# A routed transformer on one core: token tile 0 routed inside the query product, and repeated experts dropped instead of waited for

## The chip, the core and the metric

One core of one Trainium2 chip runs the whole program, in one launch. The metric is the device time of that launch in microseconds, as the median of several runs. The kernel before was run three times: 3288.59, 3291.32 and 3292.28 us, median 3291.32.

## The reference, cut to what matters

256 tokens of width 2048 go through a first block (two kinds of attention, then a routed feed-forward layer called PEER) and two further hybrid layers. All is float32. The change is in PEER alone:

```python
def peer_ffn(h, w_q, sub_keys, u, v):
    q = einsum('td,de->te', ht, w_q).reshape(T, 8, 2, 128)
    scores = einsum('thcd,hcnd->thcn', q, sub_keys)          # 8 heads, 2 halves, 128 keys
    s1, i1 = top_k(scores[:, :, 0], 16)
    s2, i2 = top_k(scores[:, :, 1], 16)
    cand_scores = (s1[..., :, None] + s2[..., None, :])       # 16 x 16 per head
    cand_idx = i1[..., :, None] * 128 + i2[..., None, :]
    top_scores, top_pos = top_k(cand_scores, 16)
    experts = take_along_axis(cand_idx, top_pos)              # 16 of 16384 per head
    gates = softmax(top_scores)
    ...
    a = einsum('td,thkd->thk', xb, u[eb])
    w = gb * gelu(a)
    return einsum('thk,thkd->td', w, v[eb])
```

Every token picks 8 x 16 = 128 experts out of 16384. Two heads of one token may pick the same expert; within one head the 16 are distinct.

## The kernel before, in words

**Weights and pieces.** The 256 tokens are two tiles of 128. All weights stream through in pieces of 1 MB (`raw`, three buffers). For each piece ScalarE (ACT) rounds it to `whi` (L155), VectorE (DVE) subtracts to get the remainder `wlo` (L156), and TensorE (PE) does three products (L180 to L182) for each of 4 row blocks and 2 token tiles, 24 matmuls in all. This L156 subtraction is called a split below, and splits are counted from the first one, which is split 0; split *n* is made two pieces ahead of its matmuls.

**What sets the order.** `chunk` runs a job of four pieces and calls `tick()` after each piece. A tick advances every running generator task by one step, in the order in which the tasks were spawned. Each engine works strictly in the program's order, so everything that a task issues between two `yield`s stands between two splits on DVE, and a row that waits holds up all rows behind it on its engine.

**The jobs around the change.** `peer_q(0..3)` (16 pieces) is the query product. After each of the four jobs, its task makes key scores for both tiles and then the top 16 of 128 for each score row (`top16`, L920 to L925; one such call is a *list*, and there are 4 lists for each job and tile). `route` is spawned after the last `peer_q`, and waits for all four. For each tile it goes through 8 heads: the 256 candidate sums (L939) and their top 16, then for each pair of heads a comparison on DVE (L955), a product on GpSimd (POOL, L959) and a reduction on DVE (L962), which give the expert's two halves. At the tile's end come the softmax, the expert numbers `ex` (L975) and the scatter addresses `au` (L977).

**The gate writes.** `scatter_gates(tt)` writes each token's gates to a dense table `gm[tt]` in DRAM: 128 indirect DMAs per tile, each issued by POOL, one column of 128 tokens per DMA (L991). Its value is the sum of the token's gates over all its copies of that expert, which DVE computes first (`same`, L1007). A tick issues four `same` and four scatters. A repeated expert is thus written more than once with the same value, at one address. Every sixteenth scatter therefore waits until the sixteen before it have landed:

```python
group.append(scatter("gates%d_%d" % (tt, k // 16), gm[tt], au[:, k:k + 1], total[:, k:k + 1],
                     group[k - 16:k] if k % 16 == 0 else ()))
```

Such a wait is called a drain below.

**Behind the gate writes.** `expert_u(0..31)` (128 pieces, splits 154 to 281) computes the activations of all experts and stores them (`wd`). `find_hits(tt)` reads `gm[tt]` back once all its 128 scatters have landed (SP issues the loads, L1026) and reduces them on DVE (L1030). After tile 1's, `list_experts` ranks the experts in use and scatters their numbers to a list `ls` in DRAM with 128 more indirect DMAs on POOL (L991 again), 4.5 per tick on average; experts not in use get an address beyond the bound (L1097, with `oob_is_err=False`, so that they are dropped). SP reads the list back (L1123) when all have landed, and DVE casts it (L1126 to L1128), before one certain split. `early_factors` multiplies gates into activations that were stored before the gates were known (L1055). Then follow `mem_kv` (8 pieces; its input tiles are rounded on ACT and subtracted on POOL, L1297, four times) and `expert_v`, whose rows POOL gathers by the list (L1185).

Of the kernel before, what the change touches and what calls it, by code (L numbers as in the profile page):

```python
# [14 lines left out]
OP = mybir.AluOpType  # L15
AX = mybir.AxisListType

P = 128
# [20 lines left out]
def tile_kernel(ctx, tc, a, o):  # L39
# [70 lines left out]
    jobs = []  # L110
# [100 lines left out]
    def pieces(ap, n=512):  # L211
        return [(ap[i], 4, n) for i in range(ap.shape[0])]
# [671 lines left out]
    def peer_q(c):  # L884


        def after(acc):
            tok = new([P, 2, 512])
            for tt in range(2):
                S.activation(tok[:, tt], acc[tt], AF.Copy, scale=st["rh"][:, tt:tt + 1])  # L890
            qT = new([P, 4, 256])

            def gen():
                yield
                transposes([[tok[:, tt, b * P:(b + 1) * P] for tt in range(2)] for b in range(4)],
                           lambda b0, nb, pt: S.copy(qT[:, b0:b0 + nb], pt))
                yield
                scs = []
                for tt in range(2):
                    p4 = psum("bs", (P, 4, P))  # L900
                    for b in range(4):
                        PE.matmul(p4[:, b], qT[:, b, tt * P:(tt + 1) * P], st["sk"][c // 2][:, 4 * (c % 2) + b],
                                  start=True, stop=True)
                    sc = new([P, 4, P])
                    S.copy(sc, p4)
                    scs.append(sc)
                yield
                for tt in range(2):
                    for b in range(4):
                        top16(slot["s"][:, tt, 4 * c + b], slot["i"][:, tt, 4 * c + b], scs[tt][:, b], P)  # L910
                        if b % 2:
                            yield
            st["pq", c] = spawn(gen())
        chunk(pieces(a["w_peer_q"][c]), lambda: st["h2"], after, before=peer_start if c == 0 else None)

    def top16(val, idx, src, n):

# [8 lines left out]

    def route():

        for c in range(4):
            while not st["pq", c].done:  # L930
                yield
        for tt in range(2):
            s, ix = slot["s"][:, tt], slot["i"][:, tt]
            ts, tp = new([P, 8, 16]), new([P, 8, 16])
            hi, lo = new([P, 8, 16]), new([P, 8, 16])
            i16 = st["iota"][:, :16]
            for h in range(8):
                cand = new([P, 16, 16])
                V.tensor_tensor(cand, s[:, 2 * h].unsqueeze(2).to_broadcast([P, 16, 16]),  # L939
                                s[:, 2 * h + 1].unsqueeze(1).to_broadcast([P, 16, 16]), op=OP.add)  # L940
# [17 lines left out]
                for which, eq in enumerate(eqs):  # L958
                    G.tensor_tensor(eq, eq, src[:, :, which].unsqueeze(2).to_broadcast([P, 2, 16, 16]), op=OP.mult)  # L959
                yield  # L960
                for eq, nm in zip(eqs, ("i1", "i2")):
                    V.tensor_reduce(slot[nm][:, tt, 16 * h0:16 * h0 + 32].rearrange("p (h k) -> p h k", h=2), eq,  # L962
                                    axis=AX.X, op=OP.add)
# [10 lines left out]
            ex, au, ad = slot["ex"][:, tt, 0], slot["au"][:, tt], new([P, P])  # L974
            V.scalar_tensor_tensor(ex, slot["i1"][:, tt], float(P), slot["i2"][:, tt], op0=OP.mult, op1=OP.add)  # L975
            V.tensor_scalar(ad, ex, float(P), st["token"], op0=OP.mult, op1=OP.add)
            V.tensor_copy(au, ad)  # L977
            st["scatter", tt] = spawn(scatter_gates(tt, ex, au, slot["ex"][:, tt, 1]))
            yield
# [17 lines left out]

    def scatter_gates(tt, ex, au, total):


        while tt and not st["scatter", 0].done:
            yield
        gt, group = slot["gt"][:, tt], []
        for k0 in range(0, P, 4):
            for k in range(k0, k0 + 4):
                same = new([P, P])
                V.scalar_tensor_tensor(same, ex, ex[:, k:k + 1], gt, op0=OP.is_equal, op1=OP.mult, accum_out=total[:, k:k + 1])  # L1007
            for k in range(k0, k0 + 4):
                group.append(scatter("gates%d_%d" % (tt, k // 16), gm[tt], au[:, k:k + 1], total[:, k:k + 1],
                                     group[k - 16:k] if k % 16 == 0 else ()))  # L1010
            yield
        yield
        st["group", tt] = group
        if tt == 0:
            st["hits"] = new([P, 2, P])
            spawn(find_hits(0, 1))

    def find_hits(tt, pace):

        yield  # L1020
        ready.append(tt)
        pend = []
        for d in range(16 + 2 * pace):
            if d < 16:
                gt = new([P, 8, P])
                after_all(nc.sync.dma_start(gt, gmp[tt][d]).ins, st["group", tt])  # L1026
                pend.append(gt)
            if d >= 2 * pace:
                e = d - 2 * pace
                V.tensor_reduce(st["hits"][:, tt, 8 * e:8 * e + 8], pend[e], axis=AX.X, op=OP.max)  # L1030
            if d % pace == pace - 1:
                yield
        st["factors", tt] = spawn(early_factors(tt))
# [586 lines left out]
    def layer(l):  # L1620
# [59 lines left out]
            chunk(pieces(w[8 + i]), xs2, z_gate(i), before=reload if i == 3 else None)  # L1680
        out2(l)

    for c in range(4):
        peer_q(c)
    jobs.append(lambda: st.__setitem__("route", spawn(route())))
    for c in range(32):
        expert_u(c)
    mem_kv(0)
# [102 lines left out]
```

## Time and profile before

| | value |
|---|---|
| median of three runs | 3291.32 us |
| the profiled execution | 3292.52 us |
| its span (first to last instruction) | 3290.7 us |
| PE busy / DVE / ACT / POOL | 95% / 59% / 45% / 34% |
| mean granted clock of PE | 0.98 |
| gate scatters on POOL | 256, mean 1312 ns |
| list scatters on POOL | 128, mean 1352 ns |

The profiled execution took 1.20 us more than the median of the runs. All times below are counted from the start of its span. A row's bracket gives the idle time of its engine just ahead of it, and what ended that; "idle before" in a grouped row is the sum of these. The work around the change lies between 860 us (query product) and 1960 us (first gathers).

### The profile page before, as it was taken

The numbers are of one execution on the slowest core, as the hardware profiler recorded it, in microseconds if no ns is written. First come the engines' busy times: TensorE is split into PE (matmuls) and PEld (weight loads), VectorE is DVE, ScalarE is ACT, GpSimd is POOL, SyncE is SP. The second block draws the span as 40 slices with busy tenths as digits, with TensorE's granted clock in tenths as the row PEclk, the third lists the DMA queues.
The fourth block names the chain that finished last, engine by engine and source line by source line (L and its number), as shares of the span: only waits on it lengthen the run. The fifth ranks groups of instructions, "written<-read, shape, count | busy, mean of one in ns | idle before, by whom it ended". The sixth has DMA issues, their size and how long they took to land. (4 is left out here: it accounts for less than half of the span.)

```text
span 3290.7 us, 38470 instructions
## 1 busy us (share of the span) xinstructions
PE 3139.9 (95%) x14755; PEld 2590.5 (79%) x14755; DVE 1935.2 (59%) x2441; ACT 1494.3 (45%) x1755; POOL 1128.1 (34%) x798
## 2 busy tenths in 40 slices
PE   8999999999999899994996899999999999999998
PEld 7888888888887778783785788887788888888886
DVE  5544455555589865861752466665675545665545
ACT  6566565443443344441442355555444443444542
POOL 1211121000002777676188688888200001000001
PEclk9999999999999999997998999999999999999999
DMA  7676455555644555993995587878644456644454
GB/s 258 203 256 223 156 183 191 204 205 204 221 167 167 175 193 171 338 321 93 371 371 208 186 293 288 287 279 302 240 177 150 164 196 239 216 157 161 153 204 154
DMA packets 172655, 717.56 MB, mean 218 GB/s; under 512 B 28865, under 2 KB 66178, under 8 KB 104114
## 3 DMA queue, kind: packets, MB, share of 16 engines
q1 hardware_dynamic: 138546, 583.57, 50.6%
q0 software_dynamic: 33920, 131.47, 11.4%
q8 instruction: 118, 1.93, 0.2%
q14 instruction: 71, 0.58, 0.0%
HBM read 659.38 MB, written 55.58 MB: 217 GB/s over the span
## 5 line engine op out<-in xcount | busy, mean ns | idle before, releaser
L156 DVE TENSOR_TENSOR wlo<-raw,whi 128x2048 fp32r<-128x2048 f32 (+3 forms) x521 | 1169.4, 2246 | 830.6 <-ACT whi L155 830.5
L181 PE MATMUL acc<-wlo,k 128*128 128x512 f32 (+3 forms) x3540 | 1372.0, 388 | 93.1 <-DVE wlo L156 93.1
L180 PE MATMUL acc<-whi,k 128*128 128x512 f32 (+3 forms) x3540 | 1398.5, 395 | 24.3 <-ACT whi L155 24.3
L182 PE MATMUL acc<-whi,k 128*128 128x512 f32 (+3 forms) x3540 | 1377.0, 389 | 0.0
L155 ACT CAST whi<-raw 128x2048 fp32r<-128x2048 f32 (+3 forms) x521 | 963.2, 1851 | 742.3 <-PE acc L182 440.4
L181 PEld LDWEIGHTS acc<-wlo,k 128*128 128x128 f32 x3540 | 671.0, 190 | 235.4 <-DVE wlo L156 100.0
L180 PEld LDWEIGHTS acc<-whi,k 128*128 128x128 f32 x3540 | 671.2, 190 | 153.6 <-ACT whi L155 24.7
L182 PEld LDWEIGHTS acc<-whi,k 128*128 128x128 f32 x3540 | 670.8, 189 | 144.6
L991 POOL DMA_INDIRECT gm<-k,k x256 | 335.8, 1312 | 138.5 <-issue 55.9
L991 POOL DMA_INDIRECT ls<-b,b x128 | 173.0, 1352 | 109.8 <-DVE b L1107 71.6
L1185 POOL DMA_INDIRECT k<-wd,b x111 | 195.1, 1757 | 37.9 <-issue 33.5
L223 POOL TENSOR_SCALAR b<-b 128x8 f32<-128x8 f32 (+1 forms) x22 | 6.9, 312 | 481.7 <-ACT b L257 241.5
L1519 POOL TENSOR_TENSOR k<-k,k 128x1024 f32<-128x1024 f32 x8 | 19.2, 2405 | 369.8 <-ACT k L1518 328.8
L1185 POOL DMA_INDIRECT raw<-peer_v_dram,b x73 | 119.4, 1636 | 46.9 <-issue 20.1
L1265 PE MATMUL acc<-whi,k 128*128 128x512 f32 x324 | 127.2, 393 | 4.7 <-DVEq L1220 3.0
L1266 PE MATMUL acc<-wlo,k 128*128 128x512 f32 x324 | 126.5, 391 | 0.0
L235 PE MATMUL bt<-ident,k 128*128 128x128 f32 x800 | 109.5, 276 | 5.5 <-DVE k L244 3.4
L156 DVE TENSOR_TENSOR wlo<-k,whi 128x2048 fp32r<-128x2048 f32 x38 | 87.1, 2292 | 41.9 <-ACT whi L155 41.8
L235 PEld LDWEIGHTS bt<-ident,k 128*128 128x128 f32 x800 | 93.9, 141 | 21.9 <-DVE k L244 4.9
L775 POOL TENSOR_TENSOR k<-k,k 128x1024 f32<-128x1024 f32 x8 | 19.3, 2415 | 262.5 <-ACT k L774 262.5
L1416 POOL COPY b<-k 128x128 f32<-128x128 f32 x4 | 8.9, 2222 | 276.5 <-DVE k L1414 276.5
L155 ACT CAST whi<-k 128x2048 fp32r<-128x2048 f32 x38 | 72.4, 1906 | 46.9 <-PE bs L1268 43.6
(363 smaller groups left out, 2803.2 us busy)
## 6 DMA issues: line engine op xcount, KB each, us to landing
raw<-w_dram SPq DMA_DIRECT2D x176, 1024.0 KB, 4.9
raw<-peer_u_dram SPq DMA_DIRECT2D x128, 1024.0 KB, 6.5
raw<-w_out_dram SPq DMA_DIRECT2D x64, 1024.0 KB, 4.8
gm<-k SPq DMA_DIRECT2D x32, 512.0 KB, 8.4
raw<-w_peer_q_dram SPq DMA_DIRECT2D x16, 1024.0 KB, 4.7
wd<-k SPq DMA_DIRECT2D x32, 512.0 KB, 7.6
k<-gm SPq DMA_DIRECT2D x32, 512.0 KB, 8.2
k<-gm SPq DMA_DIRECT2D x64, 256.0 KB, 8.1
```

The source lines that it names most:

```text
L155: S.copy(hi[:, k], r[:, k])
L156: V.tensor_sub(lo[:, k], r[:, k], hi[:, k].bitcast(F))
L180: PE.matmul(out, xh, wh, start=first, stop=False)
L181: PE.matmul(out, xh, wl, start=False, stop=False)
L182: PE.matmul(out, xl, wh, start=False, stop=last)
L235: PE.transpose(pt[:, b, tt * P:(tt + 1) * P], ins[b0 + b][tt], ident)
L775: G.tensor_tensor(z, z, y, op=OP.mult)
L991: ins = G.indirect_dma_start(dst, bass.IndirectOffsetOnAxis(ap=idx, axis=0), src, None, bounds_check=dst.shape[0] - 1, oob_is_err=False).ins
L1185: G.indirect_dma_start(dst, None, src, bass.IndirectOffsetOnAxis(ap=idx, axis=0), bounds_check=src.shape[0] - 1, oob_is_err=True)
L1265: PE.matmul(acc[n], h, hi[:, n], start=first, stop=False)
L1266: PE.matmul(acc[n], h, lo[:, n], start=False, stop=False)
L1519: G.tensor_tensor(z, z, y.rearrange("p a h d -> p a (h d)"), op=OP.mult)
```

## The change

Tile 0's lists stay with the `peer_q` tasks; tile 1's scores are kept, and its lists are made inside `route`, before each even head. `route` is spawned ahead of the first `peer_q` and waits for each job's task alone, so tile 0 is routed while the query product runs, and tile 1 beside tile 0's gate writes. Tile 1 has one more `yield` between the POOL product and the reduction.

Repeated experts are handled by address: the last 7 places of a head are compared with the next head's first 7 (49 comparisons at each of 7 borders, L988), reduced (L990), and a repeated expert's address is raised by 2^22 (L991), beyond the table's bound, so that the second write is dropped. With that the drain goes, and each scatter waits only for the one eight earlier. `scatter_gates` ends without its extra `yield`, and `find_hits` has three at its start where it had one. In the changed file the scatter is at L1006, `same` at L1021, the list read at L1136, the hits reduction at L1043, the memory subtraction at L1310.

```diff
--- before.py
+++ after.py
@@ -901,17 +901,21 @@
                     for b in range(4):
                         PE.matmul(p4[:, b], qT[:, b, tt * P:(tt + 1) * P], st["sk"][c // 2][:, 4 * (c % 2) + b],
                                   start=True, stop=True)
-                    sc = new([P, 4, P])
+                    if tt and c % 2 == 0:
+                        st["scores", c // 2] = new([P, 2, 4, P])
+                    sc = st["scores", c // 2][:, c % 2] if tt else new([P, 4, P])
                     S.copy(sc, p4)
                     scs.append(sc)
                 yield
-                for tt in range(2):
-                    for b in range(4):
-                        top16(slot["s"][:, tt, 4 * c + b], slot["i"][:, tt, 4 * c + b], scs[tt][:, b], P)
-                        if b % 2:
-                            yield
+                yield from lists(c, 0, scs[0])
             st["pq", c] = spawn(gen())
         chunk(pieces(a["w_peer_q"][c]), lambda: st["h2"], after, before=peer_start if c == 0 else None)
+
+    def lists(c, tt, sc):
+        for b in range(4):
+            top16(slot["s"][:, tt, 4 * c + b], slot["i"][:, tt, 4 * c + b], sc[:, b], P)
+            if b % 2:
+                yield
 
     def top16(val, idx, src, n):
 
@@ -926,15 +930,16 @@
 
     def route():
 
-        for c in range(4):
-            while not st["pq", c].done:
-                yield
         for tt in range(2):
             s, ix = slot["s"][:, tt], slot["i"][:, tt]
             ts, tp = new([P, 8, 16]), new([P, 8, 16])
             hi, lo = new([P, 8, 16]), new([P, 8, 16])
             i16 = st["iota"][:, :16]
             for h in range(8):
+                while ("pq", h // 2) not in st or not st["pq", h // 2].done:
+                    yield
+                if tt and h % 2 == 0:
+                    yield from lists(h // 2, 1, st["scores", h // 4][:, h // 2 % 2])
                 cand = new([P, 16, 16])
                 V.tensor_tensor(cand, s[:, 2 * h].unsqueeze(2).to_broadcast([P, 16, 16]),
                                 s[:, 2 * h + 1].unsqueeze(1).to_broadcast([P, 16, 16]), op=OP.add)
@@ -958,6 +963,8 @@
                 for which, eq in enumerate(eqs):
                     G.tensor_tensor(eq, eq, src[:, :, which].unsqueeze(2).to_broadcast([P, 2, 16, 16]), op=OP.mult)
                 yield
+                if tt:
+                    yield
                 for eq, nm in zip(eqs, ("i1", "i2")):
                     V.tensor_reduce(slot[nm][:, tt, 16 * h0:16 * h0 + 32].rearrange("p (h k) -> p h k", h=2), eq,
                                     axis=AX.X, op=OP.add)
@@ -974,6 +981,14 @@
             ex, au, ad = slot["ex"][:, tt, 0], slot["au"][:, tt], new([P, P])
             V.scalar_tensor_tensor(ex, slot["i1"][:, tt], float(P), slot["i2"][:, tt], op0=OP.mult, op1=OP.add)
             V.tensor_scalar(ad, ex, float(P), st["token"], op0=OP.mult, op1=OP.add)
+
+
+            eh, ah = (x.rearrange("p (h k) -> p h k", h=8) for x in (ex, ad))
+            eq, twice = new([P, 7, 7, 7], cls="k2"), new([P, 7, 7])
+            V.tensor_tensor(eq, eh[:, 1:8, 0:7].unsqueeze(3).to_broadcast([P, 7, 7, 7]),
+                            eh[:, 0:7, 9:16].unsqueeze(2).to_broadcast([P, 7, 7, 7]), op=OP.is_equal)
+            V.tensor_reduce(twice, eq, axis=AX.X, op=OP.max)
+            V.scalar_tensor_tensor(ah[:, 1:8, 0:7], twice, float(1 << 22), ah[:, 1:8, 0:7], op0=OP.mult, op1=OP.add)
             V.tensor_copy(au, ad)
             st["scatter", tt] = spawn(scatter_gates(tt, ex, au, slot["ex"][:, tt, 1]))
             yield
@@ -997,7 +1012,6 @@
 
     def scatter_gates(tt, ex, au, total):
 
-
         while tt and not st["scatter", 0].done:
             yield
         gt, group = slot["gt"][:, tt], []
@@ -1006,10 +1020,8 @@
                 same = new([P, P])
                 V.scalar_tensor_tensor(same, ex, ex[:, k:k + 1], gt, op0=OP.is_equal, op1=OP.mult, accum_out=total[:, k:k + 1])
             for k in range(k0, k0 + 4):
-                group.append(scatter("gates%d_%d" % (tt, k // 16), gm[tt], au[:, k:k + 1], total[:, k:k + 1],
-                                     group[k - 16:k] if k % 16 == 0 else ()))
-            yield
-        yield
+                group.append(scatter("gates%d" % tt, gm[tt], au[:, k:k + 1], total[:, k:k + 1], group[k - 8:k - 7] if k >= 8 else ()))
+            yield
         st["group", tt] = group
         if tt == 0:
             st["hits"] = new([P, 2, P])
@@ -1017,7 +1029,8 @@
 
     def find_hits(tt, pace):
 
-        yield
+        for _ in range(3):
+            yield
         ready.append(tt)
         pend = []
         for d in range(16 + 2 * pace):
@@ -1680,9 +1693,9 @@
             chunk(pieces(w[8 + i]), xs2, z_gate(i), before=reload if i == 3 else None)
         out2(l)
 
+    jobs.append(lambda: st.__setitem__("route", spawn(route())))
     for c in range(4):
         peer_q(c)
-    jobs.append(lambda: st.__setitem__("route", spawn(route())))
     for c in range(32):
         expert_u(c)
     mem_kv(0)
```

How the order moves, at three places.

DVE, from the end of tile 0's routing to its first `same`. Names are tiles with buffer numbers; `wlo` marks a split. Before:

```order
L975 SCALAR_TENSOR_TENSOR k_815_8095<-k_647_6553 128x128
L976 TENSOR_SCALAR b_817_8097<-k_815_8095,token 128x128
L977 CAST k_816_8096<-b_817_8097 128x128
L156 TENSOR_TENSOR wlo_8103<-raw_7955,whi_8102 128x2048
L939 TENSOR_TENSOR k_824_8140<-k_645_6551 128x256
L920 MAX b_820_8136<-k_824_8140 128x8
L921 MAX_INDEX b_825_8142<-b_820_8136,k_824_8140 128x8
L922 MATCH_REPLACE k_826_8143<-b_820_8136,k_824_8140 128x256
L923 MAX b_820_8136<-k_826_8143 128x8
L924 MAX_INDEX b_825_8142<-b_820_8136,k_826_8143 128x8
L925 CAST b_821_8137<-b_825_8142 128x16
L1007 SCALAR_TENSOR_TENSOR b_827_8150,k_815_8095<-k_815_8095,k_647_6553 128x128
```

and after the change:

```order
L982 SCALAR_TENSOR_TENSOR k_771_7722<-k_647_6553 128x128
L983 TENSOR_SCALAR b_773_7724<-k_771_7722,token 128x128
L988 TENSOR_TENSOR k_774_7727<-k_771_7722 128x343
L990 TENSOR_REDUCE b_775_7728<-k_774_7727 128x49
L991 SCALAR_TENSOR_TENSOR b_773_7724<-b_775_7728,b_773_7724 128x7x7
L992 CAST k_772_7723<-b_773_7724 128x128
L156 TENSOR_TENSOR wlo_7736<-raw_7591,whi_7735 128x2048
L924 MAX k_645_6551<-k_668_6799 128x8
L925 MAX_INDEX b_782_7769<-k_645_6551,k_668_6799 128x8
...
L1021 SCALAR_TENSOR_TENSOR b_788_7797,k_771_7722<-k_771_7722,k_647_6553 128x128
L156 TENSOR_TENSOR wlo_7818<-raw_7631,whi_7817 128x2048
```

The `wlo` row of the first fence is split 171 of the program, that of the second split 164, followed by two lists of tile 1 where a candidate step of tile 1 stood; the three rows L988 to L991 are new.

POOL, at the second group of sixteen of tile 0, with the semaphores waited for in brackets (DMASW0 to 7 are the eight queues of POOL's own DMAs). Before:

```order
L991 DMA gm_75<-k_815_8095,k_816_8096 2097152x1 [waits DMASW0_49,DVE_49]
L991 DMA gm_75<-k_815_8095,k_816_8096 2097152x1 [waits DMASW1_49,DVE_49]
L991 DMA gm_75<-k_815_8095,k_816_8096 2097152x1 [waits DMASW4_49,DMASW3_49,DMASW5_49,DMASW2_49,DMASW6_49,DMASW1_49,DMASW7_49,DMASW0_49,DVE_49]
L991 DMA gm_75<-k_815_8095,k_816_8096 2097152x1 [waits DVE_49] x7
L991 DMA gm_75<-k_815_8095,k_816_8096 2097152x1 [waits DMASW2_49,DVE_49]
```

and after the change:

```order
L1006 DMA gm_75<-k_771_7722,k_772_7723 2097152x1 [waits DMASW4_49,DVE_49]
L1006 DMA gm_75<-k_771_7722,k_772_7723 2097152x1 [waits DMASW5_49,DVE_49]
L1006 DMA gm_75<-k_771_7722,k_772_7723 2097152x1 [waits DMASW6_49,DVE_49]
L1006 DMA gm_75<-k_771_7722,k_772_7723 2097152x1 [waits DMASW7_49,DVE_49]
L1006 DMA gm_75<-k_771_7722,k_772_7723 2097152x1 [waits DMASW0_49,DVE_49]
```

The row that waits for all eight queues is gone; each scatter waits for one queue, that of the scatter eight earlier.

POOL, at the end of the list scatters (x77 counts scatters in a row). Before:

```order
L991 DMA ls<-b_1313_12664,b_1312_12663 16384x1 x77
L1297 TENSOR_TENSOR k_1355_13437<-k_1354_13435,k_1353_13434 128x1024
L991 DMA ls<-b_1313_12664,b_1312_12663 16384x1 x18
L1297 TENSOR_TENSOR k_1368_13659<-k_1367_13657,k_1353_13434 128x1024
L991 DMA ls<-b_1313_12664,b_1312_12663 16384x1 x18
L1297 TENSOR_TENSOR k_1378_13871<-k_1377_13869,k_1353_13434 128x1024
L991 DMA ls<-b_1313_12664,b_1312_12663 16384x1 x15
L1297 TENSOR_TENSOR k_1387_14074<-k_1386_14072,k_1353_13434 128x1024
L1185 DMA raw_14367<-peer_v_dram,b_1398_14285 128x2048
```

and after the change:

```order
L1006 DMA ls<-b_1301_12417,b_1300_12416 16384x1 x108
L1310 TENSOR_TENSOR k_1360_13562<-k_1359_13560,k_1358_13559 128x1024
L1006 DMA ls<-b_1301_12417,b_1300_12416 16384x1 x18
L1310 TENSOR_TENSOR k_1369_13764<-k_1368_13762,k_1358_13559 128x1024
L1006 DMA ls<-b_1301_12417,b_1300_12416 16384x1 x2
L1310 TENSOR_TENSOR k_1378_13957<-k_1377_13955,k_1358_13559 128x1024
L1310 TENSOR_TENSOR k_1390_14112<-k_1389_14110,k_1358_13559 128x1024
L1198 DMA raw_14365<-peer_v_dram,b_1385_14035 128x2048
```

108 list scatters instead of 77 now stand ahead of the first memory subtraction, and all 128 ahead of the third. Counted in splits, everything from the first gate scatter to the cast of the list stands 7 earlier on DVE: tile 0's hits from split 202 (before 208), tile 1's from split 235 (before 242), the last ranking step after split 246 (253), the cast of the list after split 277 (284).

## Rows read from the trace of the kernel before

**Rows 1.** The page's part on the costliest groups: line, engine, operation, tiles out<-in, count | busy us, mean ns of one | idle time of the engine just ahead of them, and what ended most of it.

```profile
L181 PE MATMUL acc<-wlo,k 128*128 128x512 f32 (+3 forms) x3540 | 1372.0, 388 | 93.1 <-DVE wlo L156 93.1
L180 PE MATMUL acc<-whi,k 128*128 128x512 f32 (+3 forms) x3540 | 1398.5, 395 | 24.3 <-ACT whi L155 24.3
...
L991 POOL DMA_INDIRECT gm<-k,k x256 | 335.8, 1312 | 138.5 <-issue 55.9
L991 POOL DMA_INDIRECT ls<-b,b x128 | 173.0, 1352 | 109.8 <-DVE b L1107 71.6
```

**Rows 2.** The timeline of PE: start us, duration us, engine, line, operation, in brackets the idle time ahead of it. The matmuls before which PE stood longest between the query product and the first gathers, and one stall of the routing (1110.92).

```profile
1110.92 0.80 PE L181 MATMUL acc<-wlo,k 128*128 128x512 f32 x1 [4.59 <-DVE wlo L156]
...
1566.60 0.79 PE L181 MATMUL acc<-wlo,k 128*128 128x512 f32 x1 [46.20 <-DVE wlo L156]
...
1769.31 0.79 PE L181 MATMUL acc<-wlo,k 128*128 128x512 f32 x1 [12.61 <-DVE wlo L156]
...
1793.96 0.80 PE L180 MATMUL acc<-whi,k 128*128 128x512 f32 x1 [12.29 <-ACT whi L155]
...
1851.96 0.79 PE L181 MATMUL acc<-wlo,k 128*128 128x512 f32 x1 [8.03 <-DVE wlo L156]
...
1885.96 0.47 PE L1265 MATMUL acc<-whi,k 128*128 128x512 f32 x1 [3.03 <-DVEq L1220]
```

**Rows 3.** The timeline of POOL: the first two gate scatters, the last two, the first list scatter, the last one, and the memory subtraction behind it.

```profile
1080.40 1.25 POOL L991 DMA_INDIRECT gm<-k,k  x1 [9.07 <-DVE b L1007]
1081.95 2.06 POOL L991 DMA_INDIRECT gm<-k,k  x1 [0.30 <-issue]
...
1553.74 0.97 POOL L991 DMA_INDIRECT gm<-k,k  x1 [0.30 <-issue]
1555.02 0.97 POOL L991 DMA_INDIRECT gm<-k,k  x1 [0.31 <-issue]
...
1627.55 1.17 POOL L991 DMA_INDIRECT ls<-b,b  x1 [71.56 <-DVE b L1107]
...
1845.09 0.97 POOL L991 DMA_INDIRECT ls<-b,b  x1 [0.30 <-issue]
1846.07 2.36 POOL L1297 TENSOR_TENSOR k<-k,k 128x1024 fp32r<-128x1024 f32 x1
```

**Rows 4.** The timeline of POOL again: six of the 14 scatters that follow a drain, the first and the last among them. The idle times of the 14, in order of time, are 1.99, 1.99, 2.00, 2.00, 2.76, 5.54, 4.93, 5.55, 7.52, 5.40, 5.71, 5.31, 2.00 and 1.99 us, 54.7 in sum.

```profile
1110.94 1.03 POOL L991 DMA_INDIRECT gm<-k,k  x1 [1.99 <-DVE wlo L156]
...
1139.95 1.03 POOL L991 DMA_INDIRECT gm<-k,k  x1 [1.99 <-DVE wlo L156]
...
1258.04 0.97 POOL L991 DMA_INDIRECT gm<-k,k  x1 [5.54 <-issue]
...
1379.61 2.71 POOL L991 DMA_INDIRECT gm<-k,k  x1 [7.52 <-DMA gm<-k,k]
...
1450.55 0.97 POOL L991 DMA_INDIRECT gm<-k,k  x1 [5.71 <-DVE b L1007]
...
1535.88 0.97 POOL L991 DMA_INDIRECT gm<-k,k  x1 [1.99 <-issue]
```

**Rows 5.** The DMA view from 1070 to 1860 us: what is written, who issued it, count, median us from issue to landing.

```profile
gm<-k,k POOLq DMA_INDIRECT x256, 5.2
ls<-b,b POOLq DMA_INDIRECT x128, 5.6
```

**Rows 6.** The timeline of DVE: splits 158 and 159 (between them two lists), 171 (behind tile 0's routing), 190, 241 and 242; then the first reduction of tile 1's hits, the first cast of the list, and split 285.

```profile
985.41 2.29 DVE L156 TENSOR_TENSOR wlo<-raw,whi 128x2048 fp32r<-128x2048 f32 x1 [1.24 <-ACT whi L155]
...
991.18 2.29 DVE L156 TENSOR_TENSOR wlo<-raw,whi 128x2048 fp32r<-128x2048 f32 x1
...
1074.64 2.29 DVE L156 TENSOR_TENSOR wlo<-raw,whi 128x2048 fp32r<-128x2048 f32 x1 [0.17 <-ACT whi L155]
...
1201.75 2.29 DVE L156 TENSOR_TENSOR wlo<-raw,whi 128x2048 fp32r<-128x2048 f32 x1
...
1499.82 2.29 DVE L156 TENSOR_TENSOR wlo<-raw,whi 128x2048 fp32r<-128x2048 f32 x1 [4.04 <-ACT whi L155]
1504.80 2.29 DVE L156 TENSOR_TENSOR wlo<-raw,whi 128x2048 fp32r<-128x2048 f32 x1 [2.08 <-ACT whi L155]
...
1561.48 1.22 DVE L1030 TENSOR_REDUCE k<-k 128x8 f32<-128x1024 f32 x1 [54.38 <-DMA k<-gm]
...
1848.96 0.23 DVE L1126 CAST b<-b 128x128 uint32<-128x128 f32 x1 [17.79 <-DMA b<-ls]
...
1849.62 2.28 DVE L156 TENSOR_TENSOR wlo<-raw,whi 128x2048 fp32r<-128x2048 f32 x1
```

**Rows 7.** The timeline of SP's queue: the first load of tile 1's hits, and the load of the list.

```profile
1557.23 0.32 SPq L1026 DMA_DIRECT2D k<-gm  x1
...
1847.27 0.33 SPq L1123 DMA_DIRECT2D b<-ls  x1
```

**Rows 8.** Groups by line, 990 to 1600 us (columns as in rows 1): DVE's comparison of a pair of heads, and its cast of the scatter addresses.

```profile
L955 DVE TENSOR_TENSOR k<-b,iota 128x512 f32<-128x512 f32 x16 | 10.3, 684 | 0.0
...
L977 DVE CAST k<-b 128x128 uint32<-128x128 f32 x2 | 0.5, 227 | 0.1
```

**Rows 9.** Windows: start:end, length, busy us (instructions) of PE, PE's weight loads, DVE, ACT and POOL, then PE's granted clock, the DMA share and GB/s.

```profile
1525.00:1550.00 25.00, 0.00 (x0) 0.00 (x0) 0.00 (x0) 0.00 (x0) 17.57 (x19) 0.50 0.02 0
1550.00:1575.00 25.00, 8.40 (x28) 6.77 (x29) 9.98 (x7) 4.89 (x4) 4.77 (x5) 0.58 0.68 251
```

## The prediction

> **What bounds the kernel now.** I first read the page's costliest groups [rows 1]. PE is busy 95% of the span, and its matmul lines name what it waits for: the remainder split on DVE, 93.1 us in all, and the rounding on ACT, 24.3 us. Both belong to the weight pieces, so the question is where a piece comes late. PE's timeline [rows 2] answers: the wait is not spread, it is one stall of 46.20 us, then 12.61, 12.29 and 8.03 us, 79.1 together. The stall of 3.03 us at 1885.96 is of another kind, and I leave it. What stood on DVE ahead of the late splits [rows 6]? At 1561.48 the first reduction of tile 1's hits, after 54.38 us of waiting for its DMA; at 1848.96 the cast of the list, after 17.79 us. Both loads are issued by SP as soon as POOL's last scatter is through: the hits at 1557.23, 1.2 us after the last gate scatter ended at 1555.99, the list at 1847.27, 1.2 us after the last list scatter ended at 1846.06 [rows 3, 7]. So POOL, with 34% busy, bounds this stretch: PE can't outrun 256 gate scatters and then 128 list scatters. The chain is
>
> - first gate scatter 1080.40 to the end of the last 1555.99: 475.6 us
> - to the first reduction of hits 1561.48: 5.5
> - ranking, to the first list scatter 1627.55: 66.1
> - to the end of the last list scatter 1846.06: 218.5
> - to PE's next matmul 1851.96: 5.9
>
> [rows 2, 3, 6]. Only what shortens this chain, or starts it earlier, helps; the same matmuls follow in any case.
>
> **Where the 475.6 us go.** In a quiet stretch a scatter takes 0.97 us with 0.30 ahead of it, 1.28 from one to the next [rows 3], or 327 us for 256. The group's busy time is 335.8 us [rows 1], 87.5 more than 256 x 0.97. The rows show where it comes from: 2.06 us at 1081.95, while the split that follows 1080.40 runs on DVE, and 0.97 after 1550, when no split runs. There are 71 splits in the stretch (172 to 242), so 1.23 us per split. The 14 drains stand 54.7 us, and would be 4.2 as common gaps, so they cost 50.5 [rows 4]. The rest, 10.4, are tile 1's products on POOL. The sum is 327 + 87.5 + 50.5 + 10.4 = 475.4.
>
> **Removed: the drains.** With the wait for eight queues gone, 475.6 becomes 425.1. But splits that fell into a drain met no scatter. The drains held 54.7 / 5.85 = 9.4 splits (5.85 us is the pace of a piece, (1499.82 - 1201.75) / 51, [rows 6]), so a split that does meet a scatter costs up to 87.5 / 62 = 1.41. I solve for the new length D: 28 pieces of tile 1's routing at an estimated 6.5 us (between the pace of 5.85 and 29.0 / 4 = 7.25, from one drain to the next in the present routing [rows 4]), the rest at 5.85. With 1.23 per split D is 423, with 1.41 it is 439; I take **431**, the middle. The wait that replaces the drain asks for the scatter 8 earlier, issued 10.2 us before at full pace; the median landing is 5.2 [rows 5], so I cost it at nothing. If that cover is gone, see the second rival.
>
> The Trainium skill bears on the terms here. "DMA: Bandwidth & Descriptors", section "Anatomy of one DMA — SWDGE (gpsimd) path", gives such a DMA a nearly constant 2.0 us, most of it the receipt; by it 14 drains would give back 14 x 1.7 = 24 us, an estimate, and the sum would be 27 longer. The trace agrees in its quiet ends (1.99), and not in the stretch where weight traffic is dense (5.54, 7.52).
>
> **Added: out-of-bounds addresses.** Three new DVE instructions per tile (the fourth piece of code only rearranges). The nearest rows are a comparison of 128x512 at 0.68 and a cast of 128x128 at 0.23 [rows 8]: between 0.7 and 2.0 us; I take 1.2, as 343 elements stand nearer to the first and the other two are small. Dropped writes: the list scatters already drop addresses beyond the bound, and take 1352 ns and land in 5.6 us, against 1312 and 5.2 [rows 1, 5], so nothing, at most 0.04 x 256 = 10 us.
>
> **Moved: tile 1's lists.** At the end of tile 0's routing DVE now has 16 lists and 7 splits fewer behind it. Two lists and a split took 991.18 - 985.41 = 5.77 [rows 6], so a list is 1.78 beside a split of 2.2: 28.5 + 15.4 - 1.2 = 42.7, and split 164 could start at 1074.64 - 42.7 = 1032. Not all of it counts, because DVE stood for ACT there (1.24 us at 985.41 [rows 6]); seven such idles give 1041 as the other end. I take 1034. A split, two lists and one `same` follow (6.1), and the first gate scatter goes out at **1040**, 40 us earlier. DVE is fuller in the query product: PE may lose about one stall of the present routing's size, 4.59 [rows 2], in a stretch that doesn't set the chain. The 28 routing pieces at 6.5 and 43 more at 5.85 bring split 235, which now stands where 242 stood, to 1034 + 182 + 251 = 1467; before, PE ran dry 15.6 us after the start of split 242 (1566.60 - 46.20 against 1504.80, [rows 2, 6]), here at 1483.
>
> **Moved: hits, list and memory tiles.** These stand seven pieces earlier on DVE and on SP, so fewer pieces are ready when the list comes, and 7 x 5.85 = 41 us of matmuls remain afterwards that were done before it. This takes back the earlier start. On POOL two of the memory subtractions of 2.36 [rows 3] stand among the list scatters instead of three: 2.4 less. SP's hit loads pass seven pieces of weight loads; they wait for the gate scatters in front of those loads, as before.
>
> **The sum.** 1040 + 431 = 1471, the last gate scatter. + 5.5 = 1476.5, first reduction, whose split lets PE go on at 1481.6 (+ 5.1, 1561.48 to 1566.60): about when PE runs dry, so the 46 us stall goes. + 64 = 1540.5, first list scatter (66.1, less an estimated 2, because PE came back from the long stall at a granted clock of 0.50 to 0.58 [rows 9], the lower level, and won't have stood here). + 216.1 = 1756.6. + 5.9 = 1762.5: PE resumes, after a single stall of some 34 us, which is what is late next (PE would run dry near 1728, 15.6 after split 277 at 1467 + 42 x 5.85 = 1713), with 7 more pieces to do: 41, and 2 for the lower clock after that stall. 1805.5 against 1851.96: **46.5 us gained**. The profiled execution took 3292.52, so 3246.0; it stood 1.2 above the median of 3291.32, so **3245** against that. Its own range: D 8 either way, the start 2 earlier or 7 later, 5 for the rest: 3232 to 3260.
>
> **Rivals.**
>
> *PE becomes the bound (3214).* If scatters stretched less without drains, the list would be in time and PE would lose nothing there: 79.1 us, with 4 for clock after two stalls, less 4.6 in the query product, is 78 gained, so 3214. It needs the list 34 us earlier (1762.5 against 1728), so D below 397. For it: without any stretch D would be 327 + 10 [rows 3]. Against: 2.06 us for a scatter beside a split, and 87.5 us in sum [rows 1, 3]. The Trainium skill's "SBUF — State Buffer", section "Who interferes with whom", speaks for it: a two-input `tensor_tensor`, such as the split, was not seen to stall the making of descriptors, so D would be near 337, an estimate. The trace doesn't agree: 2.06 against 0.97 [rows 3]. I give it 0.12.
>
> *The drain only half goes (3272).* Drains of 5 us and more lie in the stretch of dense traffic; if scatters there wait for queue room, and not for the barrier, only 14 x (1.99 - 0.30) = 23.7 goes and 26.8 stays [rows 4]: 3272. For it: 7.52 at 1379.61. Against: behind that drain scatters kept their pace. 0.13.
>
> *Slower: every split stretches more than now (3344).* Without drains, no scatter escapes a split, and a split of 2.29 may catch two. With c us per split, the sum used above is D = 327 + 10.4 + c x (28 + (D - 182) / 5.85). The gain is gone when D reaches 477.5, at c = 1.78; one scatter at its worst gives 2.71 - 0.97 = 1.74 [rows 4]. With c at 2.2, nearly the whole split, D is 530, 99 us more than forecast: 3344. It decides on one number, the mean gate scatter: above 1.5 us it is lost, against 1.31 now. Against: 1.41 at most today. 0.07.
>
> *It doesn't do what it says (3291).* The start 40 us earlier is taken back by the seven pieces (41), and if another wait on POOL, for DVE's `same` for instance, keeps the chain at 475, nothing changes. The order shows one queue's wait per scatter only, which speaks against it. 0.05.
>
> **How the numbers follow.** The forecast has 0.63. A measurement of this kernel can't tell 0.2%, 6.6 us, from no change. Faster: 0.63 + 0.12 + 0.13 = 0.88; same 0.05; slower 0.07. The range takes in the forecast and the first two rivals, each with 6 to 8 us beyond its price for the same unknowns: 3208 to 3280. No change and slower, 0.12, are left out, and some 0.08 for the tails.
>
> **What would show it.** Right: the first gate scatter near 1040 and no idle of 5 us ahead of every sixteenth; last gate scatter near 1470; mean 1.3 to 1.35 us per gate scatter; no 46 us stall, and one of 30 to 40 near 1760, behind the cast of the list; memory subtractions no longer ahead of it. Wrong: a stall still at the hits (the chain is slower than 431), none at the list (first rival), or PE losing over 10 us before 1200, where DVE now does both the lists and the routing.

## The result, and the profile after

The changed kernel takes **3247.04 us** (median of 4 runs, 3245.52 to 3248.79), against 3290.81 of the kernel before measured beside it (4 runs): ratio 0.9868, 95% interval 0.9851 to 0.9885, so 43.8 us or 1.3% faster. The forecast was 3245, in a range of 3208 to 3280. The profiled executions have spans of 3244.0 and 3290.7 us, 46.7 apart.

PE's timeline after, with the stalls that answer to [rows 2] (start us, duration us, engine, line, operation, idle time ahead of it):

```profile
1130.66 0.79 PE L181 MATMUL acc<-wlo,k 128*128 128x512 f32 x1 [6.03 <-issue]
...
1179.36 0.79 PE L181 MATMUL acc<-wlo,k 128*128 128x512 f32 x1 [6.96 <-issue]
...
1487.60 0.79 PE L181 MATMUL acc<-wlo,k 128*128 128x512 f32 x1 [10.96 <-DVE wlo L156]
...
1769.65 0.80 PE L181 MATMUL acc<-wlo,k 128*128 128x512 f32 x1 [33.84 <-DVE wlo L156]
...
1843.94 0.76 PE L1278 MATMUL acc<-whi,k 128*128 128x512 f32 x1 [3.03 <-DVEq L1233]
```

The stall of 46.20 us is down to 10.96; those of 12.61, 12.29 and 8.03 have become one of 33.84, behind the cast of the list. The last row starts 42.0 us earlier than its partner at 1885.96. The routing stalls are somewhat larger than before (4.59 was the longest, now 6.96; those over 1 us sum to 19.6 before and 24.6 after, up to 1230 us).

POOL's timeline after, for the links of the chain in [rows 3]:

```profile
1035.61 1.25 POOL L1006 DMA_INDIRECT gm<-k,k  x1 [10.70 <-DVE b L1021]
...
1475.96 0.97 POOL L1006 DMA_INDIRECT gm<-k,k  x1 [0.30 <-issue]
...
1548.96 1.17 POOL L1006 DMA_INDIRECT ls<-b,b  x1 [72.02 <-DVE b L1120]
...
1761.58 0.97 POOL L1006 DMA_INDIRECT ls<-b,b  x1 [0.30 <-issue]
1762.57 2.36 POOL L1310 TENSOR_TENSOR k<-k,k 128x1024 fp32r<-128x1024 f32 x1
```

And DVE's, for the two waits that held the splits [rows 6]:

```profile
1482.55 1.22 DVE L1043 TENSOR_REDUCE k<-k 128x8 f32<-128x1024 f32 x1 [19.24 <-DMA k<-gm]
...
1765.51 0.23 DVE L1139 CAST b<-b 128x128 uint32<-128x128 f32 x1 [41.62 <-DMA b<-ls]
```

The page's groups after, beside [rows 1]:

```profile
L181 PE MATMUL acc<-wlo,k 128*128 128x512 f32 (+3 forms) x3540 | 1367.3, 386 | 69.1 <-DVE wlo L156 52.9
L180 PE MATMUL acc<-whi,k 128*128 128x512 f32 (+3 forms) x3540 | 1395.5, 394 | 15.7 <-ACT whi L155 15.7
...
L1006 POOL DMA_INDIRECT gm<-k,k x256 | 353.4, 1380 | 88.4 <-issue 45.2
L1006 POOL DMA_INDIRECT ls<-b,b x128 | 170.3, 1330 | 110.5 <-DVE b L1120 72.0
```

The gate scatters' idle time is 88.4, of which 10.7 stands ahead of the first: 77.7 / 255 = 0.30 for each of the others. The drains are gone entirely, and the wait on the scatter 8 earlier costs nothing: behind the first scatter, one stands 0.67 us for its `same`, and no other more than 0.32. The scatters themselves became longer: 1380 ns against 1312.

### The profile page after: what moved, and what is told of

Read it like the earlier page. It is cut to its first block, busy times and chain, and to the rows that moved or that the text cites. A ratio compares the mean times of both kernels' runs of the same rounds, so it can differ in the third digit from the quotient of the medians.

```text
span 3244.0 us, 38522 instructions
## 1 busy us (share of the span) xinstructions
PE 3129.6 (96%) x14755; PEld 2583.1 (80%) x14755; DVE 1932.4 (60%) x2445; ACT 1494.0 (46%) x1755; POOL 1087.8 (34%) x798
## 5 line engine op out<-in xcount | busy, mean ns | idle before, releaser
L1006 POOL DMA_INDIRECT gm<-k,k x256 | 353.4, 1380 | 88.4 <-issue 45.2
L1006 POOL DMA_INDIRECT ls<-b,b x128 | 170.3, 1330 | 110.5 <-DVE b L1120 72.0
L1198 POOL DMA_INDIRECT k<-wd,b x111 | 174.3, 1570 | 34.5 <-issue 34.5
L1532 POOL TENSOR_TENSOR k<-k,k 128x1024 f32<-128x1024 f32 x8 | 19.2, 2406 | 369.8 <-ACT k L1531 328.8
L1198 POOL DMA_INDIRECT raw<-peer_v_dram,b x73 | 101.8, 1394 | 99.9 <-DVE wlo L156 76.2
```

Source lines behind the costliest of these rows:

```text
L1006: ins = G.indirect_dma_start(dst, bass.IndirectOffsetOnAxis(ap=idx, axis=0), src, None, bounds_check=dst.shape[0] - 1, oob_is_err=False).ins
L1198: G.indirect_dma_start(dst, None, src, bass.IndirectOffsetOnAxis(ap=idx, axis=0), bounds_check=src.shape[0] - 1, oob_is_err=True)
```

## The experiments

In the short diffs, only the lines that carry the change are shown. The times of the kernel before beside the experiments were 3290.59 us (first three) and 3289.60 (last four).

**One part at a time.** The kernel before, with the lines that raise the addresses of repeated experts (L986 to L991 of the changed file) put in, and the wait on one scatter:

```diff
-                group.append(scatter("gates%d_%d" % (tt, k // 16), gm[tt], au[:, k:k + 1], total[:, k:k + 1],
-                                     group[k - 16:k] if k % 16 == 0 else ()))
+                group.append(scatter("gates%d" % tt, gm[tt], au[:, k:k + 1], total[:, k:k + 1], group[k - 8:k - 7] if k >= 8 else ()))
```

> The kernel before with the out-of-bounds addresses and the wait on the scatter 8 earlier, its routing and yields untouched. Theory (one POOL chain sets the end; the first scatter stays at 1080, the 256 gate scatters take about 441 us as in the changed kernel, and the cast of the list stands where it stood, before split 285): last gate scatter near 1522, first list scatter near 1594, PE resumes with split 285 near 1817 instead of 1852, so about 34 us faster than before, 3253 to 3260. Rival A (the two parts add up, and the earlier start is worth its 40 us): 47 - 40 = 7 us faster, near 3284. Rival B (the drains are worth all of their 50.5 us): near 3240, faster than the changed kernel.

Measured: 3255.07 us, ratio 0.9896 (0.9878 to 0.9913), 35.5 us faster. POOL's timeline, then PE's:

```profile
1081.25 1.25 POOL L997 DMA_INDIRECT gm<-k,k  x1 [10.03 <-DVE b L1013]
...
1520.59 0.97 POOL L997 DMA_INDIRECT gm<-k,k  x1 [0.30 <-issue]
...
1593.01 1.17 POOL L997 DMA_INDIRECT ls<-b,b  x1 [71.46 <-DVE b L1112]
...
1809.03 0.97 POOL L997 DMA_INDIRECT ls<-b,b  x1 [0.30 <-issue]
```

```profile
1815.95 0.79 PE L181 MATMUL acc<-wlo,k 128*128 128x512 f32 x1 [6.80 <-DVE wlo L156]
...
1849.54 0.47 PE L1270 MATMUL acc<-whi,k 128*128 128x512 f32 x1 [3.03 <-DVEq L1225]
```

The 256 scatters take 440.3 us, the list ends at 1810.0, and PE resumed with split 285 at 1815.95 (expected 1817), 36.0 earlier than before. The theory holds to within 2 us in each link; both rivals fall.

The changed kernel with those lines taken out and the drain put back:

```diff
-                group.append(scatter("gates%d" % tt, gm[tt], au[:, k:k + 1], total[:, k:k + 1], group[k - 8:k - 7] if k >= 8 else ()))
+                group.append(scatter("gates%d_%d" % (tt, k // 16), gm[tt], au[:, k:k + 1], total[:, k:k + 1],
+                                     group[k - 16:k] if k % 16 == 0 else ()))
```

> The changed kernel with the drain of every sixteen scatters put back and the three new DVE instructions taken out; order and yields as changed. Theory (the 40 us earlier start is paid back by 7 pieces still to do after the list): first scatter near 1036, 475 us of scatters, last near 1511, PE resumes with split 278 near 1806 and has 41 to 43 us of pieces left, so 3288 to 3293, no difference from before. Rival A (the earlier start counts): about 40 us faster, near 3250. Rival B (DVE is too full in the routing and the drains fall on it too): 10 us or more slower than before, 3300.

Measured: 3288.02 us, ratio 0.9993 (0.9978 to 1.0008): no difference that can be told. POOL's timeline, the first and the last gate scatter, one that follows a drain, and the last list scatter; then PE's:

```profile
1035.44 1.25 POOL L1000 DMA_INDIRECT gm<-k,k  x1 [9.73 <-DVE b L1015]
...
1342.30 2.10 POOL L1000 DMA_INDIRECT gm<-k,k  x1 [6.84 <-DMA gm<-k,k]
...
1518.76 0.97 POOL L1000 DMA_INDIRECT gm<-k,k  x1 [0.30 <-issue]
...
1804.27 0.97 POOL L1000 DMA_INDIRECT ls<-b,b  x1 [0.30 <-issue]
```

```profile
1530.40 0.80 PE L181 MATMUL acc<-wlo,k 128*128 128x512 f32 x1 [42.39 <-DVE wlo L156]
...
1812.31 0.79 PE L181 MATMUL acc<-wlo,k 128*128 128x512 f32 x1 [33.76 <-DVE wlo L156]
...
1886.25 0.77 PE L1273 MATMUL acc<-whi,k 128*128 128x512 f32 x1 [3.03 <-DVEq L1228]
```

Its drains fell less well: the scatters took 484.3 us, not 475, so that PE resumed at 1812 and not 1806. The first scatter is 45 us earlier than before, yet the last row stands at 1886.25, where it stood at 1885.96. The list ended 41 us earlier, and PE had seven pieces (41 us) more to do behind it. So without the drop the reordering is worth nothing; its early start was turned into a stall of 33.8 us in front of work that used to be done by then. (The runs of this kernel scatter by 16 us, 3283.92 to 3299.73, and the profiled one is the longest: behind 1886 its matmuls took 397 ns in the mean from 1900 to 2280, against 391 before, at a granted clock of 0.99 to 1.00. What slows them I can't say; the rows above lie ahead of that.)

The two parts don't add up to the whole: 35.5 us and nothing, against 43.8. On top of the drop the reordering is worth 8.0 us (3255.07 against 3247.04). In both pairs about 40 us are paid back: here PE resumes 39.7 us earlier than in the kernel before and then needs 39.9 more to reach the last row; on top of the drop it resumes 46.3 earlier and needs 40.7 more. What differs is how much of the early start, 45.0 and 45.6 us, gets through to the list: here the longer drains take 8.7 of it (484.3 us against 475.6).

**Is the 34 us stall only a place?** The changed kernel, with the list loaded and cast seven ticks later:

```diff
-        yield
+        for _ in range(8):
+            yield
         lt = new([P, P])
```

> The changed kernel with seven more yields between the last list scatter and the load of the list, so that its cast stands before split 285 as in the kernel before, not 278. Theory (the 34 us stall is only the place of the cast: seven ready pieces stand behind it): PE goes on through the list scatters, the stall of 33.8 us falls under 5, the list lands at the same time near 1762, and the kernel takes about 3247 - 36 = 3211. Rival (the first gathers of the next stage then come late, because they can start no earlier): the stall moves to the first pieces of that stage and keeps 15 to 30 us, so 3225 to 3245.

Measured: 3230.79 us, ratio 0.9814 (0.9796 to 0.9832): 16 us faster than the changed kernel, not 36. The stall did go from the cast (it waits 2.20 us), but neither expectation is right: it did not move to the next stage either (the stall there is 3.03 us, as before), so that the number lies in the rival's range by another cause. PE's, ACT's and DVE's timelines:

```profile
1766.45 0.79 PE L180 MATMUL acc<-whi,k 128*128 128x512 f32 x1 [14.06 <-ACT whi L155]
...
1770.55 0.80 PE L181 MATMUL acc<-wlo,k 128*128 128x512 f32 x1 [3.30 <-DVE wlo L156]
```

```profile
1763.53 0.60 ACT L1157 ACTIVATE k<-bt 128x512 f32<-128x512 f32 x1 [26.00 <-POOL k L1311]
```

```profile
1785.88 0.23 DVE L1140 CAST b<-b 128x128 uint32<-128x128 f32 x1 [2.20 <-DMA b<-ls]
```

ACT waits 26.00 us for a tile that a memory subtraction on POOL still holds (L1311 here), and that subtraction is queued behind the list scatters. It is the same wait that gave the kernel before its stall of 12.29 us ahead of a matmul that waited for ACT [rows 2]; there ACT's timeline has

```profile
1791.04 0.60 ACT L1143 ACTIVATE k<-bt 128x512 f32<-128x512 f32 x1 [18.34 <-POOL k L1297]
```

I had counted the subtractions only for their 2.36 us on POOL.

**And if POOL has only scatters?** The same, with the four subtractions on DVE:

```diff
-            G.tensor_tensor(lo, raw, hi.bitcast(F), op=OP.subtract)
+            V.tensor_tensor(lo, raw, hi.bitcast(F), op=OP.subtract)
```

> The kernel with the late list load, and the four subtractions of the memory tiles on DVE instead of POOL. Theory (with the cast out of the way, ACT stands 26 us for a memory subtraction that is queued behind the list scatters on POOL, and this is the 17.4 us that PE still loses): the two stalls of 14.06 and 3.30 go, 3231 - 17 = 3214, perhaps 3 to 5 more where PE then reaches the cast before the list. Rival (PE then simply waits for the list at the cast, 12 us or more): 3225 or above.

Measured: 3210.34 us, ratio 0.9753 (0.9727 to 0.9778). That is 20.5 us less, where 17 were expected. Both stalls are gone, and only the one at the hits is left of those that this document follows (PE's timeline):

```profile
1487.38 0.80 PE L181 MATMUL acc<-wlo,k 128*128 128x512 f32 x1 [11.01 <-DVE wlo L156]
```

And with tile 1's hits read two ticks later:

```diff
-        for _ in range(3):
+        for _ in range(5 if tt else 3):
             yield
         ready.append(tt)
```

> The same with the hits reduction of tile 1 two ticks later (five yields instead of three at its start). Theory (the 9.7 us stall at the hits is again only the place of a wait; ranking and list scatters start at the same time, since the hits land at the same time): the stall at the hits goes, 10 us faster than the kernel without this, near 3204. Rival (ranking comes two pieces later, and the list with it, 12 us; PE loses at the list what it won at the hits): no faster than 3214.

Measured: **3197.85 us**, ratio 0.9716 (0.9691 to 0.9742), 12.5 us faster again. The stall at the hits is 2.25 us:

```profile
1489.88 0.50 PE L181 MATMUL acc<-wlo,k 128*128 128x512 f32 x1 [2.25 <-DVE wlo L156]
```

This beats both kernels, 92 us below the one before, and its scatters end no earlier than the changed kernel's (the last list scatter at 1763.1 us, against 1762.6). The difference is where the program waits for them, and that the memory subtractions no longer queue behind them.

**What stretches a scatter.** In the changed kernel a scatter alone takes 0.97 us, and some take 2 to 3. Two kernels add 32 DVE instructions of the same length, one per tick of tile 1's gate writes, with two operands or with one:

```diff
             for k in range(k0, k0 + 4):
...
+            if tt:
+                V.tensor_tensor(big, st["iota"].unsqueeze(1).to_broadcast([P, 8, P]), st["iota"].unsqueeze(1).to_broadcast([P, 8, P]), op=OP.add)
             for k in range(k0, k0 + 4):
```

```diff
             for k in range(k0, k0 + 4):
...
+            if tt:
+                V.tensor_reduce(big, st["iota"].unsqueeze(1).to_broadcast([P, 8, P]), axis=AX.X, op=OP.max)
             for k in range(k0, k0 + 4):
```

> The changed kernel with one more DVE instruction per tick of tile 1's gate writes, 32 in all: the sum of two 128x1024 operands in SBUF, into a scratch tile that nothing reads. Theory (a scatter on POOL stands still while a two-input DVE instruction runs): tile 1's 128 scatters take 214 us in the changed kernel, first start to last end; 32 instructions of about 1.15 us, of which some 60% falls on a scatter as with the splits, make it 236 us (228 to 246), and the kernel some 20 us longer, 3267. Rival (the stretching comes from the traffic of the weight loads or from chance, not from DVE): 214 us as before, 3247.

> The same with a maximum over one 128x1024 operand in SBUF instead (about 1.2 us on DVE, one input). Theory (only two-input instructions hold a scatter): tile 1's scatters take 214 us, 3247 in all. Rival (any DVE work beside a scatter stretches it): 236 us, 3267.

Measured, one run each: 3283.65 and 3246.02 us. The gate scatters' group on POOL from 1000 to 1600 us, first with two operands, then with one:

```profile
L1006 POOL DMA_INDIRECT gm<-k,k x256 | 390.3, 1525 | 88.2 <-issue 40.0 <-DVE b L1022 30.3 <-DVE k L1046 4.9
```

```profile
L1006 POOL DMA_INDIRECT gm<-k,k x256 | 352.4, 1377 | 88.2 <-issue 30.8 <-DVE b L1022 30.3 <-DVE b L1024 9.8
```

and the added instructions' group on DVE from 1200 to 1600, in the same order:

```profile
L1024 DVE TENSOR_TENSOR k<-iota 128x1024 f32<-128x1024 f32 x32 | 39.0, 1219 | 0.0
```

```profile
L1024 DVE TENSOR_REDUCE b<-iota 128x8 f32<-128x1024 f32 x32 | 38.7, 1211 | 0.0
```

39.0 us of two-operand work make the scatters 37.9 us longer than 38.7 us of one-operand work does, nearly all of it and not the 60% I expected, and the kernel is 37.6 us longer (3267 was expected): the POOL chain sets the end, one for one. DVE runs ahead of POOL, so that 6 of the 32 instructions start before tile 1's first scatter and part of the cost falls on tile 0's. The one-operand kernel equals the changed one. A stretch of the two-operand kernel shows it scatter by scatter, POOL and then DVE:

```profile
1290.03 0.97 POOL L1006 DMA_INDIRECT gm<-k,k  x1 [0.30 <-DVE k L1046]
1291.31 2.52 POOL L1006 DMA_INDIRECT gm<-k,k  x1 [0.30 <-issue]
1294.13 1.93 POOL L1006 DMA_INDIRECT gm<-k,k  x1 [0.30 <-DVE b L1022]
```

```profile
1290.69 2.29 DVE L156 TENSOR_TENSOR wlo<-raw,whi 128x2048 fp32r<-128x2048 f32 x1 [0.69 <-ACT whi L155]
...
1293.99 1.22 DVE L1024 TENSOR_TENSOR k<-iota 128x1024 f32<-128x1024 f32 x1
```

The scatter of 1291.31 starts inside the split and ends 0.85 us after the split's end at 1292.98; that of 1294.13 ends 0.85 after the added instruction's at 1295.21. In the one-operand kernel, 35 scatters run beside a reduction and nothing else; they take 0.97 us in the mean. The two added instructions also differ in what they write, 1024 elements per partition against 8, and no run separates this from the number of operands. One row speaks against it: in the kernel with the late list, a gather on POOL begins 0.33 us before the end of a DVE copy from PSUM that writes 128x512, and takes 1.02 us, where being held as other gathers are (they end 0.87 to 0.89 us behind the instruction) would make it 1.20.

## Why the prediction was right, and where its terms were off

Its mechanism is what the runs show: POOL's chain of scatters sets the end, the drains were the gain, and the earlier start is paid back by the seven pieces. The one-part experiments show the last two by themselves (35.5 us and nothing; 8.0 on top of the drop). The terms:

| step of the sum | forecast | measured |
|---|---|---|
| first gate scatter | 1040 | 1035.6 |
| the 256 gate scatters | 431 | 441.3 |
| end of the last | 1471 | 1476.9 |
| first reduction of hits | 1476.5 | 1482.6 |
| stall there | 0 | 11.0 |
| first list scatter | 1540.5 | 1549.0 |
| end of the last | 1756.6 | 1762.6 |
| PE resumes | 1762.5 | 1769.7 |
| stall at the list | 34 | 33.8 |
| more to do behind it | 43 | 40.3 |
| gain up to the next stage | 46.5 | 42.0 |

- **Start.** Split 164 came at 1029.2, not 1034, ahead of both ends of my bounds (1032 to 1041). From 860 us on, DVE had 42.6 us less work up to there, the 42.7 of the forecast, but it also stood 2.4 us less for other engines, where I allowed for up to 9 more. The three new DVE instructions took 0.51, 0.51 and 0.21 us, the 1.2 of the forecast.
- **The scatters' length** was mis-sized by 10 us and lay 2 beyond my upper end. I priced a split at 1.23 to 1.41 us and took the middle; after the change it costs (353.4 - 248.3) / 71 = 1.48, if all of the stretching is put down to splits. Counted one by one, 60 of the 71 splits held a scatter before, for 1.39 us each, and all 71 do after, for 1.42 (the other 4 us lie beside shorter two-operand instructions). So what a split costs hardly changed; with the drains gone it always meets a scatter, which it holds to its own end. That was in the prediction as the upper value, and should have been its forecast. The mean, 1380 ns, lies above the 1.3 to 1.35 us that I named as a sign. My third rival was this mechanism, and its worst scatter, 2.71 us, was only the worst of the rows shown: the longest of the kernel before took 3.05. It decides at 477.5 us, and two_input reached 478.1 and stood at 3283.65, not far from no gain.
- **Hits.** The 6 us later and a PE that ran dry at 1476.6 instead of 1483 make the stall of 11 us that I had at zero. I had named such a stall as a sign of being wrong, of a chain slower than 431, and the chain was. It costs nothing in the sum, since the chain behind it is unchanged. The ranking took 66.4, as before (66.1): the 2 us that I took off for the clock were not there.
- **The list.** 213.6 us against 216.1; its scatters were also stretched a little less (1330 ns against 1352). From its end to PE's next matmul it is 7.1 us, not 5.9: a DVE instruction of 1.22 us (L1161), whose partner ran behind the split before, now stands between the cast and the split.
- **Dropped writes** were costed at nothing, and that fits: 60 gate scatters with no DVE instruction beside them take 0.97 us in the mean, as 96 did before (how many of the 60 drop a write, the traces don't tell).
- **Where the other microseconds come from.** The gain is 42.0 at the end of this stage, and 46.7 in the spans. The rest arises in the gathers. Before, PE waited twice at their end; these two rows of the kernel before have no partner over 1.2 us after (the drop alone keeps both, at 1.75 and 1.90; the reordering alone has neither):

```profile
2299.90 0.50 PE L1265 MATMUL acc<-whi,k 128*128 128x512 f32 x1 [1.68 <-ACT k L1200]
...
2338.64 0.68 PE L1266 MATMUL bt<-wlo,k 128*128 128x512 f32 x1 [2.43 <-DVE wlo L156]
```

I had not looked at that stage at all. That the total came within 2 us of the forecast is therefore partly luck: two errors of over 4 us cancel.

The first rival (PE becomes the bound) needed the 256 scatters in under 397 us; they took 441.3, and two_input confirms the reading of the 2.06 us row that spoke against it. The second (the drain half goes) fell: no scatter behind the first waits more than 0.67. Of my signs, "PE losing over 10 us before 1200" was badly put: it loses 19.2 us there in stalls over 1 us, but 19.6 before as well.

The clock plays its part, too. Two pairs of windows that end at the same matmul (the last row of PE's timeline above), from 950 and from 1500 us on, each before and then after (start:end, length, busy of PE, PEld, DVE, ACT, POOL, granted clock, DMA share, GB/s):

```profile
950.00:1886.00 936.00, 826.47 (x3671) 675.18 (x3669) 581.21 (x1190) 357.40 (x294) 566.70 (x417) 0.94 0.68 234
...
1500.00:1886.00 386.00, 300.34 (x1331) 244.85 (x1329) 171.71 (x134) 128.52 (x104) 241.72 (x185) 0.89 0.69 244
```

```profile
950.00:1844.00 894.00, 816.95 (x3670) 667.65 (x3668) 584.45 (x1223) 357.76 (x294) 571.75 (x415) 0.96 0.72 245
...
1500.00:1844.00 344.00, 304.47 (x1377) 249.29 (x1376) 169.29 (x129) 136.59 (x111) 197.46 (x145) 0.94 0.80 274
```

From 1500 us on, 46 more matmuls fit into 42 us less, and PE is busy only 4 us longer for them: it stalls for less time, and works less at the lower of its two levels, 1.2 GHz (a mean granted clock of 0.94 against 0.89). From 950 us on, the work is the same but for one matmul. PE stands 109.5 us before (936.00 - 826.47) and 77.1 after, so 32.5 of the 42 us are stalls; the other 9.5 are matmuls that ran shorter, at a mean granted clock of 0.96 against 0.94.

## What to carry to other kernels

Starting a chain earlier helps only if the wait at its end does not move forward with it: when a reordering shifts the start and the place of the waiting instruction by the same number of pieces, most of its gain is paid back (here some 40 us out of 40 and out of 46), and the free gain lies in moving the wait back: 16 us here for the list's wait alone, 49 with the hits' wait moved and the memory subtractions taken off POOL as well. When a slow queue sets the end, look at what shares it: four short subtractions behind 128 scatters held ACT and PE for 17 us. And count what a faster engine will now meet: the scatters freed of their drains ran into every split.

## What the runs showed of the hardware

An indirect scatter that POOL begins while a two-operand DVE instruction on SBUF runs is held until that instruction ends: in the changed kernel each of the 71 splits holds one, and it ends 0.84 to 0.89 us behind the split. A scatter that began before the split is not held (0.97 us at 1290.03 above). 32 instructions of 1.22 us made the scatters 37.9 us longer than 32 one-operand ones of 1.21 did, which cost nothing; that the operands decide, and not what is written, rests on the one row named there. The gathers behave alike: before, the 130 of 222 that begin beside such an instruction take 2.24 us in the mean, the others 1.01. Before and with the drop alone the 222 took 1.73 and 1.72 us in the mean, in the changed kernel 1.50, where 30 of them waited for a split's end (94.0 us of idle on POOL) and all but one of these then took 1.00 to 1.09. The Trainium skill's "SBUF — State Buffer", section "Who interferes with whom", says that a DVE instruction with two SBUF inputs contends with a GpSimd instruction that reads SBUF, and in the same section that `tensor_tensor` was not seen to stall a DMA. The first fits these rows; the second does not hold for these indirect DMAs, whose addresses lie in SBUF (that reading them is what waits is an inference). Why the gathers fall into one pattern or the other stays open.
